# TensorE's order in the scans of a two-layer encoder written out by the program, and the first layer's score products made of 128-row passes

## The chip, the core and the metric

The kernel runs on one core of one Trainium2 chip. The metric is the device time of one execution in microseconds (us), as the median of several runs. Instructions go to engines with queues of their own: TensorE (PE in the profile; its weight loads are PEld), VectorE (DVE), ScalarE (ACT), GpSimd (POOL), and SyncE (SP), which here issues the DMAs.

## The reference: what is computed

Two sequences, 512 and 256 tokens of width 1024, go through a trunk of two layers with shared weights.

- Layer 0 mixes tokens by dilated sliding-window attention (8 heads of 64) beside a short gated convolution. Layer 1 mixes them by RWKV-7 time mixing: 16 heads of 64, a forward and a backward scan, summed.
- Each layer then adds a cross-attention over 256 memory tokens (4 heads of 256) and a SwiGLU of inner width 2816. RMS norms stand before every part and at the end.

The scan that gives layer 1 its shape is, per head and token,

```
S_t = S_{t-1} diag(w_t) + (S_{t-1} a_t) b_t^T + v_t k_t^T ;  o_t = S_t r_t
```

## The kernel before, in words

**Numbers.** Activations lie with features on the 128 partitions and tokens along the free axis. Each fp32 operand of a large product is split into a rounded part `hi` and a remainder `lo`, and a product is three passes on TensorE: hi·hi, hi·lo, lo·hi (`mms`, lines 330 to 341, and `products`, lines 324 to 328).

**Weights outside the scans.** `wcols` (lines 250 to 274) loads up to 2048 weight columns per partition, then splits a tile of 1024 into `whi` on ScalarE (line 269) and `wlo` on VectorE (line 270), with three buffers each.

**The stages, in order.** `mixer0` (layer 0's mixer, lines 617 to 770), `ca` (cross-attention), `ffn`, `mixer1` (layer 1's mixer, lines 1439 to 1486), `ca`, `ffn`. In the profiled execution the scans of `mixer1` lie from 1267 to 2325 us.

**Layer 0's scores.** In `attend` (lines 680 to 725) a head's query and key lie on 64 of the 128 partitions. For each of 4 pairs of heads, 2 heads and 6 blocks of 128 queries (4 of the first sequence with 512 keys, 2 of the second with 256 keys) line 708 makes the three passes over 64 rows. That is 48 sites.

**The scans.** The work of `mixer1_scan` (lines 1041 to 1413) is cut into 12 units, of two heads of the first sequence or four of the second. Four generators do a unit's work in turns: `prep` (decays, keys, norms; its products are line 1073 by `wide` and lines 1025 and 1038 by `head_rsqrt`), `inverse` (the triangular inverses: products of line 1179, then the 32-row products of lines 1223, 1229, 1248 and 1257, with a chain of small VectorE operations between), `scan`, and `tail`. `weave` (line 1535) gives turns in proportion to a count. Beside unit u's scan stand the inverse of unit u+1, the tail of u-1 and the prep of u+2 (line 1404).

**A scan step.** There are 8 steps a unit, 96 in all. `C<-uv,G` and `C<-S,ar` make P; ScalarE copies it to R (line 1328); `C<-R,Xinv` makes U; ScalarE and VectorE copy it to uv (lines 1331 and 1332); `C<-uv,BT` makes Z, which VectorE adds into the state S (line 1343); `y<-G,uv` and `y<-ar,S` make the output. So a step has three round trips from TensorE to another engine and back.

**Fill.** Other dense products (the second sequence's SwiGLU of layer 0, its inputs to the scan, memory keys, the first sequence's output product) are a generator `fill` of some 480 pieces, each of six passes of 256 columns or three of 512. `pour` (line 1279) draws them three times a step.

**What sets TensorE's order.** The program is traced in the order of the turns, and then a scheduler orders each engine's instructions by a simulated timeline; the engine executes that order. Before, the one constraint in the scans is `tc.issue_after`: a piece drawn by `pour` is not issued before the scan's last product traced so far. Everything else may be moved and interleaved.

## Time and profile before

| what | value |
|---|---|
| median of 3 runs (lowest to highest) | 3078.29 us (3075.21 to 3082.93) |
| the profiled execution, its own time | 3090.49 us |
| its span, first to last instruction | 3088.7 us |
| mean granted TensorE clock, share of 2.4 GHz | 0.97 |
| busy share TensorE / weight loads / VectorE / ScalarE / GpSimd | 96 / 81 / 54 / 40 / 21 % |

A line of a group names the source line, engine, operation, output<-inputs, shape and count, then the busy time, the mean length of one, and the idle time just before it with what ended it. Matmuls are pipelined: a 512-column pass is shown some 0.39 us long, but the next starts well before its end. So lengths are not added up; starts are compared. The granted clock has two levels here, 1.0 (2.4 GHz) and 0.5 (1.2 GHz), and a window shows their mean.

### The profile page before, as it was taken

The page shows a single profiled execution, that of the slowest core. Times are in us where ns is not written, and L with a number is a line of the kernel's source. Part 1 is how long each engine was busy: PE and PEld are TensorE (multiplying, and loading weights), DVE is VectorE, ACT ScalarE, POOL GpSimd, SP SyncE. Part 2 cuts the span into 40 slices and gives each one's busy share as a digit, 9 for nine tenths or more (in the row PEclk, how much of TensorE's full clock was granted, in tenths as well). Part 3 has the DMA queues.
Part 4 walks back from the last instruction along what each step waited for, and adds up shares of the span by engine and source line. Part 5 has one row for each costly group of instructions (what it writes and reads, how often), then busy time and mean ns, then how long its engine had stood idle before and what let it go on. Part 6 is the DMA issues. An engine that isn't in the chain of part 4 may idle for free.

```text
span 3088.7 us, 54824 instructions
## 1 busy us (share of the span) xinstructions
PE 2961.8 (96%) x22672; PEld 2487.1 (81%) x22672; DVE 1664.4 (54%) x2762; ACT 1234.2 (40%) x2253; POOL 663.7 (21%) x664
## 2 busy tenths in 40 slices
PE   7999999999999989899989999999999999999997
PEld 6888888888888878787778777777778888888886
DVE  8678646464454486455576455444436464334244
ACT  3232435332222366455556565555345332112112
POOL 3113004020000110232364234444245020000001
PEclk9999999999999989999999899999899999999998
DMA  3114333111265666764435453222352112212211
GB/s 117 49 58 127 102 107 95 65 55 55 97 208 180 210 195 229 237 200 144 139 110 163 137 151 100 76 80 66 107 174 94 53 41 71 66 55 69 69 55 55
DMA packets 349275, 344.46 MB, mean 112 GB/s; under 512 B 40929, under 2 KB 287841, under 8 KB 349025
## 3 DMA queue, kind: packets, MB, share of 16 engines
q1 hardware_dynamic: 349024, 340.96, 34.7%
q8 instruction: 178, 2.92, 0.4%
q14 instruction: 73, 0.59, 0.1%
HBM read 269.06 MB, written 71.83 MB: 110 GB/s over the span
## 4 chain that ended last, share of the span: by engine, by line
PE 81%; DVE 8%; DMA 4%; ACT 3%; issue 2%; POOL 1%; SPq 0%; POOLq 0%; DVEq 0%; ACTq 0%
PE mm L337 22%; PE mm L338 21%; PE mm L339 21%; PE C L1288 3%; PE g L1179 3%; PE sm L328 2%; PE y L1288 2%; PE e L1073 2%; DVE lt L1204 1%; DVE xr L1205 1%; PE py L328 1%; PE mm L328 1%; DMA tlo<-low 1%; DMA traw<-in_ffn_wgu_dram 1%; DVE xs L232 1%
## 5 line engine op out<-in xcount | busy, mean ns | idle before, releaser
L337 PE MATMUL mm<-xs,whi 128*128 128x512 f32 x2128 | 754.0, 356 | 29.4 <-ACT whi L269 11.7
L338 PE MATMUL mm<-xs,whi 128*128 128x512 f32 x2128 | 754.0, 354 | 3.6 <-DVE xs L232 2.7
L339 PE MATMUL mm<-xs,wlo 128*128 128x512 f32 x2128 | 749.5, 352 | 2.4 <-DVE wlo L270 2.3
L269 ACT CAST whi<-wraw 128x1024 fp32r<-128x1024 f32 (+1 forms) x246 | 256.1, 1043 | 781.4 <-PE mm L338 742.9
L337 PEld LDWEIGHTS mm<-xs,whi 128*128 128x128 f32 x2128 | 404.0, 190 | 93.7 <-ACT whi L269 12.3
L339 PEld LDWEIGHTS mm<-xs,wlo 128*128 128x128 f32 x2128 | 402.5, 189 | 62.5 <-DVE wlo L270 4.2
L338 PEld LDWEIGHTS mm<-xs,whi 128*128 128x128 f32 x2128 | 403.6, 190 | 59.3 <-DVE xs L232 3.4
L196 POOL TENSOR_TENSOR acc<-acc,sq 128x768 f32<-128x768 f32 (+2 forms) x72 | 123.2, 1711 | 1388.6 <-issue 896.0
L270 DVE TENSOR_TENSOR wlo<-wraw,whi 128x1024 fp32r<-128x1024 f32 (+1 forms) x246 | 309.3, 1260 | 164.5 <-ACT whi L269 156.3
L338 PE MATMUL mm<-fb,thi 128*128 128x256 f32 (+1 forms) x720 | 235.3, 327 | 1.8 <-DVE fb L229 1.8
L338 PE MATMUL mm<-hid,whi 128*128 128x512 f32 (+1 forms) x528 | 188.6, 358 | 0.0
L337 PE MATMUL mm<-hid,whi 128*128 128x512 f32 (+1 forms) x528 | 186.5, 356 | 1.9 <-ACT hid L228 1.9
L339 PE MATMUL mm<-hid,wlo 128*128 128x512 f32 (+1 forms) x528 | 187.0, 355 | 0.0
L337 PE MATMUL mm<-fb,thi 128*128 128x256 f32 x528 | 166.4, 316 | 6.0 <-ACT thi L298 5.9
L298 ACT CAST thi<-traw 128x512 fp32r<-128x512 f32 (+1 forms) x202 | 122.8, 609 | 115.5 <-PE mm L338 63.7
L339 PE MATMUL mm<-fb,tlo 128*128 128x256 f32 x528 | 156.0, 297 | 8.6 <-POOL tlo L302 4.0
L378 DVE SCALAR_TENSOR_TENSOR u<-mm,rstd 128x768 f32<-128x768 f32 (+1 forms) x44 | 38.4, 873 | 211.6 <-PE mm L339 211.6
L338 PEld LDWEIGHTS mm<-fb,thi 128*128 128x128 f32 x720 | 143.9, 200 | 9.3 <-issue 3.6
L398 DVE TENSOR_TENSOR x<-x,mm 128x512 f32<-128x512 f32 (+2 forms) x56 | 42.4, 762 | 173.6 <-PE mm L339 173.5
L337 PE MATMUL mm<-fa,thi 128*128 128x512 f32 (+1 forms) x304 | 128.9, 426 | 0.8 <-ACT fa L228 0.6
L337 PEld LDWEIGHTS mm<-fb,thi 128*128 128x128 f32 x528 | 105.6, 200 | 17.1 <-ACT thi L298 8.6
L339 PE MATMUL mm<-fa,tlo 128*128 128x512 f32 (+1 forms) x304 | 114.1, 375 | 1.7 <-DMA tlo<-low 1.7
(373 smaller groups left out, 5850.8 us busy)
## 6 DMA issues: line engine op xcount, KB each, us to landing
wraw<-in_ffn_wgu_dram SPq DMA_DIRECT2D x44, 1024.0 KB, 5.1
tlo<-low SPq DMA_DIRECT2D x128, 256.0 KB, 3.2
low<-wlo SPq DMA_DIRECT2D x60, 512.0 KB, 3.2
wraw<-in_ffn_wdown_dram SPq DMA_DIRECT2D x23, 1024.0 KB, 5.2
traw<-in_ffn_wgu_dram SPq DMA_DIRECT2D x56, 256.0 KB, 3.5
wraw<-in_ab_w_in_dram SPq DMA_DIRECT2D x24, 512.0 KB, 3.8
wraw<-in_ca_wkv_dram SPq DMA_DIRECT2D x8, 1024.0 KB, 5.5
kvd<-kv SPq DMA_DIRECT2D x32, 256.0 KB, 2.0
```

The costliest lines, as they stand in the source:

```text
L196: nc.gpsimd.tensor_add(acc, acc, sq)
L269: nc.scalar.copy(hi[:, :, :m], raw[:, :, j:j + m])
L270: nc.vector.tensor_sub(lo[:, :, :m], raw[:, :, j:j + m], hi[:, :, :m].bitcast(F32))
L298: nc.scalar.copy(hi[:, :n], raw[:, :n])
L328: self.nc.tensor.matmul(ps, lhsT=a[u], rhs=b[v], start=k == 0 and j == 0, stop=k == len(pairs) - 1 and j == 2)
L337: nc.tensor.matmul(ps[:, s0:s1], lhsT=wh, rhs=xh[:, s0:s1], start=start and k == 0, stop=False)
L338: nc.tensor.matmul(ps[:, s0:s1], lhsT=wh, rhs=xl[:, s0:s1], start=False, stop=False)
L339: nc.tensor.matmul(ps[:, s0:s1], lhsT=wl, rhs=xh[:, s0:s1], start=False, stop=stop and k == n - 1)
L398: self.nc.vector.tensor_add(self.x[m], self.x[m], ps)
L1073: nc.tensor.matmul(ps[:, c], lhsT=l, rhs=r, start=True, stop=True)
L1179: nc.tensor.matmul(ps[h][:, j, d, :], lhsT=flat(BK[d][lohi[h], c]), rhs=flat(AR[d][lohi[h], c]), start=True, stop=True)
L1288: last[0] = nc.tensor.matmul(o, lhsT=lhsT, rhs=rhs, start=start, stop=False, skip_group_check=True)
```

## The change

- In the scans every TensorE instruction is tied behind the one traced before it (`keep_in_program_order`), so the order of turns and of statements is the order that TensorE executes. `pin` is on only around `mixer1_scan`.
- For that order the generators are cut finer: `head_rsqrt` yields between its sum and its transposes, `prep` yields once more, the scan's transposes of values and keys are apart, `mem_kv` yields before its transposes. `pour` draws two shares between P and U and one at each of the two other places, of 32 a unit instead of 24.
- Layer 0's scores: of a head's query, `hi` stays on the head's 64 rows and the remainder goes by DMA to the other 64 rows; the key's `hi` and `lo` are copied by DMA to both halves. Two passes over 128 rows take the place of three over 64 (the lo·lo term comes in too).
- `wcols` splits a weight tile in two halves with four buffers each (two whole tiles instead of three); a one-row-block load takes 512 columns instead of 1024. `mixer0` draws the weights of the next product ahead of the current one.
- Two tables are moved or shrunk (`gmu`, `rstd`), which is not shown.

```diff
@@ class Net
+    def matmul(self, *args, **kw):
+        return self.pinned(self.nc.tensor.matmul(*args, **kw))
...
+    def pinned(self, ins):
+        if self.pin[0]:
+            self.tc.keep_in_program_order(ins)
+        return ins
...
@@ def wcols
-        W = min(n, 2048 // nk // 128 * 128)
-        cw = min(W, 1024 // nk // 128 * 128)
+        W = min(n, 2048 // nk // 128 * 128 if nk > 1 else 512)
+        cw = min(W, 1024 // max(2, nk) // 128 * 128)
...
-                hi = self.wp.tile([128, nk, cw], F32R, name="whi", bufs=3)
-                lo = self.wp.tile([128, nk, cw], F32R, name="wlo", bufs=3)
-                nc.scalar.copy(hi[:, :, :m], raw[:, :, j:j + m])
-                nc.vector.tensor_sub(lo[:, :, :m], raw[:, :, j:j + m], hi[:, :, :m].bitcast(F32))
+                parts = []
+                for k0 in range(0, nk, -(-nk // 2)):
+                    k1 = min(nk, k0 - (-nk // 2))
+                    hi = self.wp.tile([128, k1 - k0, cw], F32R, name="whi", bufs=4)
+                    lo = self.wp.tile([128, k1 - k0, cw], F32R, name="wlo", bufs=4)
+                    nc.scalar.copy(hi[:, :, :m], raw[:, k0:k1, j:j + m])
+                    nc.vector.tensor_sub(lo[:, :, :m], raw[:, k0:k1, j:j + m], hi[:, :, :m].bitcast(F32))
+                    parts.append((k0, k1, hi, lo))
...
@@ def mem_kv
             if m >= KT:
+                yield
                 p2 = self.sm(4, 128)
@@ def mixer0
+        cols = [1024, *head(0), *keyq(1), 1152, *head(1), *keyq(2), None, *head(2), 1280, *keyq(3), *head(3), None, 1408]
+        made = {}
+        def make():
+            c = cols.pop(0) if cols else None
+            if c is not None:
+                made[c] = next(self.wcols(w_in, 0, 8, c, 128))
...
         def product(col, tag="mm", **kw):
             ps = self.pmm.tile([128, T], F32, name=tag, **kw)
-            self.mm(ps, next(self.wcols(w_in, 0, 8, col, 128)), xs)
+            if col not in made:
+                make()
+            w = made.pop(col)
+            make()
+            self.mm(ps, w, xs)
...
-            hi, lo = self.pair("qk", 8)
-            nc.scalar.copy(hi, z)
-            nc.gpsimd.tensor_sub(lo, z, hi.bitcast(F32))
-            return hi, lo
+            return z
+        def half(z, to, rest):
+            for t, r, rows in zip(to, rest, heads):
+                nc.scalar.copy(t[rows], z[rows])
+                nc.gpsimd.tensor_sub(r[rows], z[rows], t[rows].bitcast(F32))
+        def other(t, h, src):
+            nc.sync.dma_start(t[heads[1 - h]].bitcast(F32), src)
...
         def keys(p, o):
+            z = rotary(proj(512 + p * 128))
+            hi = [self.ph.tile([128, T], F32R, name="qk", bufs=12) for _ in heads]
+            lo = [self.ph.tile([128, T], F32R, name="qk", bufs=12) for _ in heads]
+            half(z, hi, lo)
+            for h, rows in enumerate(heads):
+                for t in (hi[h], lo[h]):
+                    other(t, h, t[rows].bitcast(F32))
...
+            z = rotary(proj(p * 128, 0.125))
+            o["q"] = [self.ph.tile([128, T], F32R, name="qk", bufs=12) for _ in heads]
+            half(z, o["q"], [z, z])
+            for h, t in enumerate(o["q"]):
+                other(t, h, z[heads[h]])
@@ attend
-                        self.products(ps[:, :n], [([a[hs, c:c + 128] for a in q], [a[hs, s0:s1] for a in k])])
+                        for j, kt in enumerate(k[h]):
+                            self.matmul(ps[:, :n], lhsT=q[h][:, c:c + 128], rhs=kt[:, s0:s1], start=j == 0, stop=j == 1)
@@ def head_rsqrt
         nc.scalar.copy(bc, y[:, :8].rearrange("p (t h) -> p t h", h=2).unsqueeze(3).to_broadcast([128, 4, 2, 64]))
+        yield
         out = pool.tile([128, 512], F32, name="e")
@@ mixer1_scan, prep
                 rks.append((c, rk))
+            yield
@@ mixer1_scan, scan
-            def pour():
-                todo[0] += rate[2 + u] / 24
+            def pour(n):
+                todo[0] += n * rate[2 + u] / 32
                 while todo[0] >= 1:
                     todo[0] -= 1
-                    with tc.issue_after(last[0].ins):
-                        next(fill, None)
+                    next(fill, None)
...
-            nxt = ahead(0)
+            uv = values(0)
+            yield
+            bt = keys(0)
             yield
...
-                    pour()
+                    pour(2)
                     R = ph.tile([128, 128], F32, name="R", bufs=1)
...
-                    pour()
+                    if j and i + 1 < NG:
+                        bt2 = keys(i + 1)
+                    pour(1)
                     yield
...
                     if j == 0 and i + 1 < NG:
-                        nxt = ahead(i + 1)
-                    pour()
+                        uv2 = values(i + 1)
+                    pour(1)
...
@@ mixer1_scan
-            weave((part(scan, u), 17), (part(inverse, u + 1), 16), (part(tail, u - 1), 4), (part(prep, u + 2), 12))
+            weave((part(scan, u), 18), (part(inverse, u + 1), 16), (part(tail, u - 1), 5), (part(prep, u + 2), 14))
@@ mixer1
+                    self.pin[0] = True
                     y = self.mixer1_scan(L, rkv, zs, bvs, self.fill(l, f, xsave, rkv, L, zs))
+                    self.pin[0] = False
```

## Rows read from the trace of the kernel before

**Rows 1.** Timeline of TensorE, a dense stretch: start, length, instruction.

```profile
1220.21 0.39 PE L338 MATMUL mm<-xs,whi 128*128 128x512 f32 x1
1220.44 0.39 PE L339 MATMUL mm<-xs,wlo 128*128 128x512 f32 x1
```

**Rows 2.** Windows: us, busy time of each engine, granted clock, DMA share, GB/s.

```profile
0.00:630.00 630.00, 612.12 (x3456) 517.89 (x3457) 422.99 (x738) 223.07 (x344) 119.38 (x84) 1.00 0.28 88
...
1267.00:2325.00 1058.00, 986.59 (x11899) 796.89 (x11897) 558.36 (x1214) 583.38 (x1315) 425.60 (x488) 0.93 0.44 131
```

**Rows 3.** Waits of TensorE, 1267 to 2325 us: us in total, times, longest.

```profile
PE C L1288 <- DVE S L1343: 6.4, 10, 1.3
PE g L1248 <- DVE X L1231: 6.4, 4, 2.4
...
PE C L1288 <- DVE uv L1332: 5.4, 6, 2.0
...
PE y L1288 <- ACT uv L1331: 4.4, 7, 1.3
PE C L1288 <- ACT R L1328: 4.2, 7, 1.1
...
PE mm L181 <- DVE bc L175: 3.1, 2, 2.7
```

**Rows 4.** Groups by line, shapes kept apart: the first layer's scores, line 328.

```profile
L328 PE MATMUL sm<-qk 64*128 64x512 f32 x96 | 30.5, 425 | 0.0
...
L328 PE MATMUL sm<-qk 64*128 64x256 f32 x48 | 10.1, 314 | 0.3 <-DVE mx L711 0.3
```

**Rows 5.** Timeline of TensorE, two score sites.

```profile
228.25 0.62 PE L328 MATMUL sm<-qk 64*128 64x256 f32 x3
228.79 0.50 PE L337 MATMUL mm<-xs,whi 128*128 128x512 f32 x1
...
256.37 0.96 PE L328 MATMUL sm<-qk 64*128 64x512 f32 x3
257.26 0.39 PE L337 MATMUL mm<-xs,whi 128*128 128x256 f32 x1
```

**Rows 6.** Timeline of TensorE in the scans, dense fill and cut runs.

```profile
1630.96 0.28 PE L337 MATMUL mm<-fb,thi 128*128 128x256 f32 x1
1631.08 0.28 PE L338 MATMUL mm<-fb,thi 128*128 128x256 f32 x1
1631.29 1.71 PE L1179 MATMUL g<-ar,bk 64*128 64x128 f32 x16
1632.93 0.34 PE L1288 MATMUL y<-G,uv 128*64 128x64 f32 x4
...
1635.05 0.48 PE L1179 MATMUL g<-ar,bk 64*128 64x128 f32 x2
1635.47 0.39 PE L338 MATMUL mm<-fb,thi 128*128 128x256 f32 x1
1635.69 0.28 PE L339 MATMUL mm<-fb,tlo 128*128 128x256 f32 x1
1635.90 0.71 PE L1179 MATMUL g<-ar,bk 64*128 64x128 f32 x4
```

**Rows 7.** Timeline: first and last run of L1179, then of L1223 to L1257.

```profile
1301.82 0.48 PE L1179 MATMUL g<-ar,bk 64*128 64x128 f32 x2
...
2195.67 2.08 PE L1179 MATMUL g<-ar,bk 64*128 64x128 f32 x10
...
1356.04 1.29 PE L1223 MATMUL g<-X,G 32*32 32x32 f32 x128 [0.63 <-DVE X L1213]
...
2239.58 0.43 PE L1257 MATMUL g<-Xinv,Y 32*32 32x32 f32 x14
```

**Rows 8.** The page, part 5: the split of a weight tile.

```profile
L269 ACT CAST whi<-wraw 128x1024 fp32r<-128x1024 f32 (+1 forms) x246 | 256.1, 1043 | 781.4 <-PE mm L338 742.9
```

**Rows 9.** The page, part 6: DMA issues, KB each, us to landing.

```profile
tlo<-low SPq DMA_DIRECT2D x128, 256.0 KB, 3.2
```

More of the change, by code (lines that the diff above doesn't have):

```diff
@@ L45, in __init__ @@
         self.W, self.seqs = T, SEQS
[L46 removed]
+        self.slots, self.wide, self.pin = None, False, [False]
         self.open_x()
@@ L205, in rstd @@
             for i, s in enumerate(acc):
-                nc.tensor.matmul(ps[:, t:t + 1], lhsT=s[:, t * 128:(t + 1) * 128], rhs=self.ones,
+                self.matmul(ps[:, t:t + 1], lhsT=s[:, t * 128:(t + 1) * 128], rhs=self.ones,
                                  start=i == 0, stop=i == len(acc) - 1)
@@ L327, in products @@
             for j, (u, v) in enumerate(((0, 0), (0, 1), (1, 0))):
-                self.nc.tensor.matmul(ps, lhsT=a[u], rhs=b[v], start=k == 0 and j == 0, stop=k == len(pairs) - 1 and j == 2)
+                self.matmul(ps, lhsT=a[u], rhs=b[v], start=k == 0 and j == 0, stop=k == len(pairs) - 1 and j == 2)
     def mms(self, ps, w, xs, start=True, stop=True):
@@ L336, in mms @@
             for s0, s1 in self.seqs:
-                nc.tensor.matmul(ps[:, s0:s1], lhsT=wh, rhs=xh[:, s0:s1], start=start and k == 0, stop=False)
-                nc.tensor.matmul(ps[:, s0:s1], lhsT=wh, rhs=xl[:, s0:s1], start=False, stop=False)
-                nc.tensor.matmul(ps[:, s0:s1], lhsT=wl, rhs=xh[:, s0:s1], start=False, stop=stop and k == n - 1)
+                self.matmul(ps[:, s0:s1], lhsT=wh, rhs=xh[:, s0:s1], start=start and k == 0, stop=False)
+                self.matmul(ps[:, s0:s1], lhsT=wh, rhs=xl[:, s0:s1], start=False, stop=False)
+                self.matmul(ps[:, s0:s1], lhsT=wl, rhs=xh[:, s0:s1], start=False, stop=stop and k == n - 1)
             if (k + 1) % PIECE[self.W] == 0 and k + 1 < n:
@@ L628, in mixer0 @@
             nc.sync.dma_start(self.rot[i], a["rot"][i])
+        head = lambda p: [2048 + 128 * p, 2560 + 128 * p, 1536 + 128 * p]
+        keyq = lambda p: [512 + 128 * p, 128 * p]
+        cols = [1024, *head(0), *keyq(1), 1152, *head(1), *keyq(2), None, *head(2), 1280, *keyq(3), *head(3), None, 1408]
[5 more added lines that the diff above has]
+        make()
         def product(col, tag="mm", **kw):
             ps = self.pmm.tile([128, T], F32, name=tag, **kw)
-            self.mm(ps, next(self.wcols(w_in, 0, 8, col, 128)), xs)
+            if col not in made:
+                make()
+            w = made.pop(col)
+            make()
+            self.mm(ps, w, xs)
             return ps
@@ L1047, in mixer1_scan @@
         units += [(1, [(p, slice(0, 256)), (p + 1, slice(256, 512))]) for p in range(0, 8, 2)]
-        last, tc = [None], self.tc
         steps = ([(s, s, 0, s, 7 - s) for s in range(8)],
@@ L1072, in wide @@
             for (c, l), r in zip(lhsT, rhs):
-                nc.tensor.matmul(ps[:, c], lhsT=l, rhs=r, start=True, stop=True)
+                self.matmul(ps[:, c], lhsT=l, rhs=r, start=True, stop=True)
             return ps
@@ L1126, in prep @@
                     nkk = kk
-                    rn = self.head_rsqrt(sq, 0.0, 1.0, 1e-24, t6, self.pp)
-                    nc.vector.scalar_tensor_tensor(nkk, kk, -1.0, rn, op0=OP.mult, op1=OP.mult)
+                    rn = []
+                    yield from self.head_rsqrt(sq, 0.0, 1.0, 1e-24, t6, self.pp, rn)
+                    nc.vector.scalar_tensor_tensor(nkk, kk, -1.0, rn[0], op0=OP.mult, op1=OP.mult)
                 yield
@@ L1277, in scan, with values @@
             todo = [0]
-            def pour():
-                todo[0] += rate[2 + u] / 24
+            def pour(n):
+                todo[0] += n * rate[2 + u] / 32
                 while todo[0] >= 1:
                     todo[0] -= 1
-                    with tc.issue_after(last[0].ins):
-                        next(fill, None)
+                    next(fill, None)
             def mm(o, lhsT, rhs, start=False):
-                last[0] = nc.tensor.matmul(o, lhsT=lhsT, rhs=rhs, start=start, stop=False, skip_group_check=True)
-            def ahead(i):
+                self.matmul(o, lhsT=lhsT, rhs=rhs, start=start, stop=False, skip_group_check=True)
+            def values(i):
                 g = st[2 * i:2 * i + 2]
@@ L1381, in tail @@
             yield
-            nc.vector.tensor_mul(y, y, self.head_rsqrt(sq, 64e-5, 1.0 / 64, None, tt, self.pp))
+            rn = []
+            yield from self.head_rsqrt(sq, 64e-5, 1.0 / 64, None, tt, self.pp, rn)
+            nc.vector.tensor_mul(y, y, rn[0])
             for p, c in parts:
@@ L1400, in mixer1_scan @@
         rate = [n * r / sum(f) for n, f in zip(self.fill_len(), FILL) for r in f]
-        weave((part(prep, 0), 12), more(rate[0]))
-        weave((part(inverse, 0), 16), (part(prep, 1), 12), more(rate[1]))
+        weave((part(prep, 0), 14), more(rate[0]))
+        weave((part(inverse, 0), 16), (part(prep, 1), 14), more(rate[1]))
         for u in range(NU + 1):
-            weave((part(scan, u), 17), (part(inverse, u + 1), 16), (part(tail, u - 1), 4), (part(prep, u + 2), 12))
+            weave((part(scan, u), 18), (part(inverse, u + 1), 16), (part(tail, u - 1), 5), (part(prep, u + 2), 14))
         for _ in fill:
```

69 lines of the change are left out of this document (39 added, 30 removed).

## The prediction

> **What bounds the kernel now.** I read the page's busy shares first: TensorE is busy nearly all of the span and no other engine is near it. Busy time of pipelined passes says little: a dense 512-column pass is shown 0.39 us long, but the next starts 0.23 us after it [rows 1]. So the windows by stage came next. In layer 0's mixer the clock is full and TensorE's idle time is small; in the scans, 1267 to 2325 us, TensorE is idle for 1058.0 - 986.6 = 71 us, and its clock is 0.93 on average, which costs (1 - 0.93) x 1058 = 74 us of work not done [rows 2]. The waits say what the 71 us are: many short ones, none of which dominates [rows 3]. They are of three kinds. Round trips of a scan step (S, both uv, R) make 6.4 + 5.4 + 4.4 + 4.2 = 20.4 us in 30 waits, 0.68 us each; products of the inverse wait 6.4 us for X; the fill waits for split weights, and 3.1 us for a norm's spread.
>
> The third loss is in no wait. In the timeline a fill pass of 256 columns starts 0.12 us after the one before, and 16 line 1179 records in one run take 1632.93 - 1631.29 = 1.64 us, 0.10 each. Cut out as two records they take 1635.47 - 1635.05 = 0.42 us instead of 0.21; the fill pass behind them takes 0.22, and the one ahead of the next cut 0.21, instead of 0.12 [rows 6]. So an excursion of two records from the fill and back costs 0.21 + 0.10 + 0.09 = 0.4 us that no wait explains. The scheduler makes many: the timeline of 1267 to 2325 us has line 1179 in 92 separate runs (first and last shown) and the 32-row products in 110 [rows 7].
>
> **The change, part by part.** The sum is made against the profiled execution, 3090.5 us, which is 12.2 us above the median of the runs.
>
> *Layer 0's scores: -16.* There are (96 + 48) / 3 = 48 sites, 32 of 512 columns and 16 of 256 [rows 4]. Three 64-row passes hold TensorE for 257.26 - 256.37 = 0.89 us and 228.79 - 228.25 = 0.54 us [rows 5]. Two 128-row passes at the pitch of dense passes, 0.23 [rows 1] and 0.12 [rows 6], are 0.46 and 0.24. The saving is 32 x 0.43 + 16 x 0.30 = 18.6 us. The lowest it can be is one pass of each site, 32 x 0.23 + 16 x 0.12 = 9.3. The stage is TensorE's: VectorE has 423 of 630 us [rows 2], so it counts. Against it stand 24 DMAs inside the core, one more ScalarE copy and one more GpSimd subtraction for each of 8 keys and queries. GpSimd has 119 of 630 us and ScalarE 223 [rows 2]; both have room. A transfer's nearest price is 3.2 us to landing [rows 9]; for pairs 1 to 3 attention of the pair before hides it, for pair 0 the convolution's products do, unless they have run out: 0 to 5 us. I take 3, so -16, bounds -19 and -4. SP's queue carries the 24 DMAs among loads issued well ahead.
>
> *Weight tiles in halves, drawn ahead: 0.* A split lasts 1.04 us [rows 8]; a stage's first product can start after half of it, some 0.5 us at each of a few starts. Each half pays a start of its own on ScalarE and VectorE, hidden beside TensorE outside the scans. Two tiles of room instead of three leave about one product, 24 passes or more of 0.23 us, to prepare the next; that covers a split. The exception is line 877, which opens three columns at once; with room for two the third starts later. -3 to +6, I take 0.
>
> *Order in the scans, fewer runs: -33.* Laid out in the order of turns, line 1179 makes one run of 16 records for each of 4 turns in 12 units, 48, and the 32-row products one run for each of 4 turns, 48. That removes 44 and 62 runs. 44 x 0.4 = 18 us by the row above. For the 32-row runs no clean pair of rows stands here; the lower end is 0.1 (one slower start), the upper 0.4, and I take 0.25 since many lie beside other small products: 15 us. Bounds -11 (0.1 for each of 106) and -42.
>
> *Order in the scans, waits: -12.* Now every wait holds all that follows, so I count the cover that the new order writes down. Between P and U stand two fill pieces, 12 x 0.12 = 1.4 us; between U and Z one piece, 0.7 us, and on average two turns of the other generators; between Z and the next step the output products and another piece. A round trip that fails now fails by 0.68 us on average [rows 3], so 0.7 to 1.4 us of certain cover should end at least half of them: -10. The inverse's products get a turn or more of distance: -7 from the inverse's waits, of which X is the largest. The weight waits stay: the same buffers feed the fill. New ones: the norm inside `small_low` must now be followed at once by its transposes, +3 by the price of the same helper at the start [rows 3]; and the one bank that `prep` and `tail` share can be asked for in neighbouring turns, +2. Sum -12. Bounds: -45 if all but the weight waits go; above, what the rival below says.
>
> *The clock: -17.* The clock's 74 us follow from the waits. Listing the low stretches behind the idle times over 1 us, about half of the low time (68 of some 140 us at the low level) stands behind waits of steps and inverses. If half of those go, 68 / 2 / 2 = 17 us come back. Bounds -47 (in proportion to all waits that could go, 45 of 71) and 0.
>
> Sum: -16 + 0 - 33 - 12 - 17 = **-78 us**, 3012 against the profile's 3090.5, and 3078.3 - 78 = **3000 us** against the median.
>
> **Where a page and the rows differ.** The Trainium skill (TensorEngine Tiling (Array Packing), section Tiling Modes, under Key Properties) says that changing the tiling mode drains TensorE. The traces agree at both places used above: 64-row passes are slow at their edges in rows 5 and in rows 6. By that rule alone only changes of the active rows or columns would count, and not every broken run. They number 726 in the timeline of the scans and 562 in the new order; at 0.1 us, an estimate from the fill's slower starts, the runs would give -16 instead of -33 and the total 3017.
>
> **The rivals.**
>
> *All waits covered.* If the written order covers every round trip, the terms are -19 - 42 - 45 - 47 = -153: 2925 us. For it: the cover of 0.7 to 1.4 us exceeds the mean wait. Against it: the copies wait in ScalarE's and VectorE's queues behind other work, and those two queues are still ordered by the simulated timeline.
>
> *Waits at the head (slower).* The place is the step's round trips, 96 x 3 = 288. If ScalarE or VectorE come to a copy late, nothing later can pass it now. The price is 0.68 us each [rows 3], and about half as much again in clock. A third of all trips waiting, beyond those that wait today, is 96 x 0.68 x 1.5 = 98 us, against -16 - 33 = -49: 3127 us. It decides from 49 / 1.02 = 48 more waits, one trip in six. For it: VectorE runs 558 of 1058 us and the inverse's chain must fit among the rest [rows 2]; the scheduler chose its order to avoid just these waits in its simulation. Against it: 30 of 288 wait today in an order that was simulated with durations that need not be the chip's, with no cover written down.
>
> *The order hardly changes.* If the scheduler's order was close to the program's, only layer 0's part is left: 3062 us. The cuts of two and four records [rows 6] speak against it.
>
> **How the numbers follow.** The forecast gets 0.55, its own range is 2950 to 3060. All waits covered: 0.16. Order hardly changed: 0.08. Waits at the head: 0.17. The remaining 0.04 is gains and losses that cancel. About 0.3%, 9 us, is what a measurement of this kernel can tell from no change. Faster by more: nearly all of the first, all of the second, most of the third, 0.76. Slower: 0.17. Same: 0.07. The range for 8 in 10 reaches down to the second case's centre, which leaves out 0.07, and up to 3095, which leaves out the larger part of the slow case, 0.13: 2925 to 3095.
>
> **What would show it.** Right: the score sites as pairs of 128-row passes with no slow start behind them; line 1179 in 48 runs of 16; fewer and shorter waits of line 1288; a mean clock in the scans of 0.95 or more; the scans shorter by some 60 us and layer 0's mixer by some 16. Wrong: waits of line 1288 for R, uv or S that together exceed 50 us, a clock at or below 0.93, or a wait for a score's copied half at the first pair. The prediction fails if the scans are as long as before though line 1179 stands in 48 runs: then cuts cost less than the rows say, or new waits took their place.

## The result and the profile after

The changed kernel takes 3119.5 us (median of 4 runs, 3113.7 to 3120.9), the kernel before 3080.6 us in runs beside it: a ratio of 1.0125, 95% interval 1.0105 to 1.0145. It is slower by 39 us, where I had forecast 78 us less. Its profiled execution took 3113.7 us, its span is 3111.9 us, so profile against profile the loss is 23 us; the profiled execution of before lay some 10 us above its median, this one 6 below. Times are medians; one slow run of four of f6_pairs_free_order, 5078.1 us, is left out.

The granted clock of whole runs goes with the two figures. It was 0.970 in the profiled execution of before, where the runs of that kernel recorded with the experiments have 0.974 on average, and 0.971 in this one, where its four runs have 0.967. So the two profiles show the same clock, while over the runs the changed kernel loses up to (0.974 - 0.967) x 3100 = 22 us more to it, an estimate from the clocks of the runs.

The windows of the changed kernel, layer 0's mixer and the scans (us, then busy time of TensorE, weight loads, VectorE, ScalarE, GpSimd, granted clock, DMA share, GB/s):

```profile
0.00:620.00 620.00, 589.53 (x3391) 511.32 (x3392) 434.38 (x798) 238.81 (x412) 132.32 (x91) 0.99 0.32 97
1250.00:2350.00 1100.00, 929.82 (x11918) 754.84 (x11917) 556.03 (x1220) 582.83 (x1319) 428.37 (x489) 0.94 0.42 126
```

Beside [rows 2], TensorE is idle for 170 us in the scans instead of 71, and the clock of the profiled execution is what it was. The waits of TensorE in the same stretch (all its products now carry line 52 and its transposes line 55, the lines of the helpers, so the tiles tell them apart) name the idle time:

```profile
PE C L52 <- ACT R L1396: 41.7, 24, 4.6
PE C L52 <- DVE uv L1400: 33.2, 30, 4.1
PE e L55 <- DVE rs_w L1091: 11.9, 7, 5.3
PE g L52 <- DVE X L1276: 11.1, 6, 8.0
...
PE mm L52 <- ACT thi L313: 9.6, 4, 7.9
PE e L55 <- ACT bc L1096: 8.9, 6, 3.6
```

Against [rows 3], the wait for R has gone from 4.2 us in 7 to 41.7 us in 24, the one for uv from VectorE from 5.4 us in 6 to 33.2 us in 30.

**Where the time went.** I cut every trace at the same two places: the start of the norm that opens the scan stage and the end of the last fill product. Of the stage in between, three things can be counted: the time in which TensorE does nothing, half of its busy time at the low clock level (1.2 GHz, summed from the stretches of the granted clock), and the rest, which is its work at 2.4 GHz.

| us | start of stage | length | idle | low clock, half | rest | behind it |
|---|---|---|---|---|---|---|
| before | 1267.0 | 1065.0 | 71.4 | 66.5 | 927.1 | 756.7 |
| changed | 1250.6 | 1103.7 | 170.2 | 57.5 | 875.9 | 757.7 |
| difference | -16.4 | +38.6 | +98.8 | -9.0 | -51.2 | +1.0 |

-16.4 + 38.6 + 1.0 = 23.2 us, the difference of the spans. So the change shortened TensorE's work more than I had said, and new waits took twice of that back. The low level itself lasted 139.9 us in both stages; its half is 9 us less only because TensorE is idle for more of it.

**Why R comes late.** In a timeline of the changed kernel (start, length, instruction, in brackets the idle time before it and what ended it):

```profile
1833.82 0.39 PE L52 MATMUL C<-S,ar 128*64 128x128 f32 x4
...
1835.31 0.40 PE L52 MATMUL mm<-fb,thi 128*128 128x256 f32 x2
1835.54 0.28 PE L52 MATMUL mm<-fb,tlo 128*128 128x256 f32 x1
1835.91 0.62 ACT L1337 COPY v<-v 128x512 f32<-128x512 f32 x1 [4.59 <-DMA v<-v]
1836.54 2.50 ACT L1304 COPY Xinv<-XL 32x512 f32<-32x512 f32 x4
1839.06 0.69 ACT L1171 ACTIVATE th<-e,half 128x512 f32<-128x512 f32 x1
1839.65 0.26 ACT L1396 COPY R<-C 128x128 f32<-128x128 f32 x1
...
1839.96 0.66 PE L52 MATMUL C<-R,Xinv 128*128 128x64 f32 x4 [4.14 <-ACT R L1396]
```

P is done at 1834.2 us and the fill behind it covers the trip until 1835.8. But ScalarE has stood for 4.59 us before the copy of v, which waits for its DMA; then come four copies of Xinv and a tanh, and R only behind them. In 11 of the 12 units the copy of v stands so ahead of one R, in ten of them with all four copies of Xinv and the tanh, and R starts 3.1 to 5.4 us after P is done. The 11 waits make 32.9 of the 41.7 us. ScalarE's order is still made by the simulated timeline, presumably with v landed sooner (not shown); the order of TensorE is not, so nothing that could run meanwhile is allowed ahead of `C<-R,Xinv`.

### The profile page after: what moved, and what is told of

It reads as the page before. It is cut to its first block, busy times and chain, and to the rows that moved or that the text cites. A ratio compares the mean times of both kernels' runs of the same rounds, so it can differ in the third digit from the quotient of the medians.

```text
span 3111.9 us, 55784 instructions
## 1 busy us (share of the span) xinstructions
PE 2877.7 (92%) x22624; PEld 2437.0 (78%) x22624; DVE 1691.9 (54%) x3008; ACT 1279.3 (41%) x2507; POOL 670.7 (22%) x672
## 5 line engine op out<-in xcount | busy, mean ns | idle before, releaser
L52 PE MATMUL mm<-xs,whi 128*128 128x512 f32 (+1 forms) x4256 | 1132.0, 354 | 14.9 <-ACT whi L281 11.0
L281 ACT CAST whi<-wraw 128x512 fp32r<-128x512 f32 (+1 forms) x492 | 301.5, 616 | 840.4 <-PE mm L52 791.9
L282 DVE TENSOR_TENSOR wlo<-wraw,whi 128x512 fp32r<-128x512 f32 (+1 forms) x492 | 364.8, 743 | 390.1 <-ACT whi L281 352.3
L52 PE MATMUL mm<-hid,whi 128*128 128x512 f32 (+1 forms) x1056 | 282.0, 356 | 2.3 <-ACT hid L236 2.3
L52 PEld LDWEIGHTS mm<-hid,whi 128*128 128x128 f32 x1056 | 186.2, 189 | 31.8 <-ACT hid L236 2.7
L52 PE MATMUL mm<-fa,thi 128*128 128x256 f32 (+1 forms) x416 | 140.1, 387 | 5.0 <-ACT fa L452 3.4
L52 PE MATMUL mm<-o,whi 128*128 128x512 f32 (+1 forms) x512 | 130.1, 342 | 2.8 <-DVE x L590 1.1
L52 PEld LDWEIGHTS mm<-fb,tlo 128*128 128x128 f32 x528 | 106.9, 203 | 8.7 <-DMA tlo<-low 4.8
L52 PEld LDWEIGHTS mm<-hid,wlo 128*128 128x128 f32 x528 | 99.3, 188 | 14.7
L52 PEld LDWEIGHTS mm<-o,whi 128*128 128x128 f32 x512 | 88.3, 189 | 15.9 <-DVE o L237 2.3
L52 PE MATMUL C<-R,Xinv 128*128 128x64 f32 x384 | 58.1, 276 | 41.8 <-ACT R L1396 41.7
```

The lines of the kernel that those rows point to most:

```text
L52: return self.pinned(self.nc.tensor.matmul(*args, **kw))
L281: nc.scalar.copy(hi[:, :, :m], raw[:, k0:k1, j:j + m])
L282: nc.vector.tensor_sub(lo[:, :, :m], raw[:, k0:k1, j:j + m], hi[:, :, :m].bitcast(F32))
```

## The experiments

Ratios are against the kernel before on the same chip. Idle time, low clock and rest are those of the stage, from each kernel's one trace; "clock" is the mean granted clock of all its runs, over the whole execution (before: 0.974), where 0.001 is 3 us; "pairs" is explained under the third question.

| kernel | us | ratio, 95% interval | clock | stage | idle | low | rest | pairs |
|---|---|---|---|---|---|---|---|---|
| changed | 3119.5 | 1.0125 (1.0105 to 1.0145) | 0.967 | 1103.7 | 170.2 | 57.5 | 875.9 | 370 |
| e2_layer0_alone | 3051.1 | 0.9909 (0.9884 to 0.9934) | 0.978 | 1042.6 | 61.5 | 55.0 | 926.1 | 166 |
| e9_weights_alone | 3067.6 | 0.9977 (0.9962 to 0.9993) | 0.977 | 1042.7 | 62.4 | 52.7 | 927.6 | 161 |
| e1_order_free | 3094.8 | 1.0056 (1.0032 to 1.0079) | 0.965 | 1082.2 | 77.5 | 78.7 | 925.9 | 142 |
| e4_pin_alone | 3304.6 | 1.0728 (1.0696 to 1.0760) | 0.936 | 1297.4 | 265.9 | 163.3 | 868.3 | 384 |
| e3_v_on_gpsimd | 3087.1 | 1.0031 (1.0014 to 1.0048) | 0.972 | 1082.1 | 149.8 | 57.0 | 875.3 | 374 |
| e5_two_copies_tied | 3077.0 | 0.9996 (0.9976 to 1.0016) | 0.973 | 1067.7 | 137.2 | 56.0 | 874.5 | 374 |
| e6_scalar_in_order | 3161.0 | 1.0287 (1.0240 to 1.0335) | 0.955 | 1153.4 | 177.7 | 105.0 | 870.7 | 378 |
| e7_scalar_vector_in_order | 3212.2 | 1.0433 (1.0397 to 1.0469) | 0.949 | 1206.9 | 208.2 | 130.5 | 868.2 | 376 |
| g1_uv_on_scalar | 3062.6 | 0.9941 (0.9919 to 0.9963) | 0.974 | 1050.8 | 131.6 | 43.0 | 876.2 | 376 |
| f2_cover_for_uv | 3111.8 | 1.0132 (1.0097 to 1.0167) | 0.968 | 1111.1 | 158.6 | 78.7 | 873.8 | 378 |
| f3_norm_yield | 3092.7 | 1.0067 (1.0041 to 1.0093) | 0.969 | 1081.9 | 149.8 | 61.0 | 871.1 | 378 |
| f4_cover_yield_priority | 3134.6 | 1.0198 (1.0164 to 1.0232) | 0.959 | 1129.3 | 156.3 | 106.1 | 867.0 | 376 |
| f1_runs_by_priority | 3037.6 | 0.9889 (0.9851 to 0.9927) | 0.977 | 1027.2 | 63.2 | 45.4 | 918.5 | 127 |
| f8_pairs_apart | 3148.4 | 1.0217 (1.0186 to 1.0248) | 0.963 | 1125.6 | 154.2 | 79.5 | 891.9 | 140 |
| f6_pairs_free_order | 3046.2 | 0.9877 (0.9840 to 0.9913) | 0.978 | 1038.8 | 86.7 | 50.2 | 902.0 | 370 |
| f5_pairs_and_priority | 3038.8 | 0.9868 (0.9844 to 0.9892) | 0.977 | 1029.0 | 91.5 | 50.2 | 887.3 | 382 |
| g2_free_pairs_tied | 3063.9 | 0.9935 (0.9914 to 0.9956) | 0.972 | 1051.4 | 107.8 | 57.8 | 885.8 | 372 |

### First question: which part of the change costs?

**e1_order_free.** The finer cuts stay, the order of TensorE is given back to the scheduler.

```diff
-                    self.pin[0] = True
+                    self.pin[0] = False
...
-                    next(fill, None)
+                    with tc.issue_after(last[0].ins):
+                        next(fill, None)
```

> The changed kernel with TensorE's order in the scans left to the scheduler again (fill pieces tied only behind the scan's last product, as before); the finer cuts and all of layer 0's part stay. Theory A (the fixed order itself costs: TensorE stands at each product whose operand a copy on ScalarE or VectorE brings late, and nothing later may pass): its idle time in the scans falls from 170 us to near the 71 us of before, and the time to 3060 us (3045 to 3080). Theory B (the finer cuts and the other shares of the turns cost, not the order): it stays at 3105 to 3130 us.

Measured 3094.8 us, between the two theories. The fixed order itself costs 25 us net (3119.5 - 3094.8; 21 by the ratios); in the trace, rest and idle time are back near their values of before (925.9 and 77.5 us), as theory A has it. That the time doesn't follow is mostly the clock: 0.965 over the runs.

**e2_layer0_alone.** `mem_kv`, `head_rsqrt`, `mixer1_scan` and `fill_len` are those of before; all else is the change's. **e9_weights_alone.** The same, and the three 64-row passes of before besides, so that of the change only the weight tiles and the moved tables are left.

> The scans as before, everything outside them as changed (128-row passes, halved weight tiles, weights drawn ahead). By the prediction's term and theory A: 16 us faster than before, 3064 us (3055 to 3075), with the scans as long as before. Theory C (the halves and the copies give back what the passes save): 3078 us or more, and then the scans cost less than theory A says.

> The scans of before and the three 64-row passes of before; only the weight tiles in halves, the weights drawn ahead and the moved tables of the change are in. My prediction had 0 for this part (-3 to +6) and -16 for the two 128-row passes. If that split holds, the first norm of the scan stage starts at 1264 to 1270 us (before 1267.0, with the passes 1246.8) and the time is 3070 to 3085 us. If the halves carry part of the gain, the start is under 1260. The scan stage itself has the code of before: if the order of the simulated timeline is the reason why it was 22 us shorter with the passes (1042.6 against 1065.0 us), its length here may be anything between 1040 and 1080.

The first product of the stage tells the layer's part. In the timelines of e9_weights_alone and of e2_layer0_alone:

```profile
1264.72 0.50 PE L52 MATMUL mm<-ones,acc 128*128 128x1 f32 x4
```

```profile
1246.84 0.50 PE L52 MATMUL mm<-ones,acc 128*128 128x1 f32 x4
```

Weights: 1267.0 - 1264.7 = 2.3 us. Passes: 1264.7 - 1246.8 = 17.9 us. Two score sites of the changed kernel show why:

```profile
236.32 0.41 PE L52 MATMUL sm<-qk 128*128 128x256 f32 x2
236.56 0.38 PE L55 MATMUL sm<-ident,e 128*128 128x128 f32 x2
...
253.85 0.63 PE L52 MATMUL sm<-qk 128*128 128x512 f32 x2
254.31 0.28 PE L52 MATMUL mm<-xs,whi 128*128 128x256 f32 x1
```

254.31 - 253.85 = 0.46 us and 236.56 - 236.32 = 0.24 us, where three passes held 0.89 and 0.54 [rows 5].

The stage of e9_weights_alone, whose scans have the code of before, is 22 us shorter than in the profile of before at the same rest (927.6 and 927.1). All of it is idle time and clock. Part is the execution that was profiled (the ratio allows -2 to -12 us for the whole kernel); the order that the simulation makes moves a little whenever anything around it changes. So idle time and clock of a free order are known to some 15 us here, the rest to about 2. The starts of the kernels with all that the change does ahead of the stage lie between 1245.3 and 1250.6 us, so the 2.3 us of the weights are no more than the scatter.

The 44 us of e1_order_free over e2_layer0_alone are idle time (+16) and clock (+24 in the traces), in the same rest. The clock is more than the scatter of one trace here: 0.965 over 10 runs beside 0.978 over 4, up to 40 us. Which of the finer cuts brings this wasn't tried.

**e4_pin_alone.** The coarse scans of before with TensorE's order fixed.

```diff
+                    self.pin[0] = True
...
-                    with tc.issue_after(last[0].ins):
-                        next(fill, None)
+                    next(fill, None)
```

> The scans of before, cut as coarsely as before, with TensorE's order fixed; outside the scans as changed. Theory A: without the finer cuts the fixed order waits more often than in the changed kernel, since sums and transposes of one norm then stand next to each other and a step has 1.4 pieces at each place: 3140 to 3220 us. Theory B: the cuts are what costs, so 3090 us or less.

3304.6 us: 253 more than the same kernel with its order free, and beyond what I expected. The stage has 204 us more idle time, 108 more of low clock and 58 less of the rest. The waits of TensorE:

```profile
PE e L55 <- ACT bc L1095: 83.3, 23, 5.3
PE e L55 <- ACT uv L1359: 70.2, 48, 3.7
```

The first is the norm whose transposes follow their sum at once, the second the keys' transposes, which need the PSUM bank that ScalarE is still emptying for uv. In the changed kernel, which has yields at both places, 11.9 + 8.9 us are left of the norm's and 2.3 us of the bank's. So the finer cuts are needed for a fixed order; how much each does wasn't taken apart.

### Second question: whose waits are the 99 us?

**e3_v_on_gpsimd**, **e5_two_copies_tied** and **e6_scalar_in_order** take hold of ScalarE's queue at three widths.

```diff
-                nc.scalar.copy(v2[:, b, 0, :], v[:, ::-1, ::-1])
+                nc.gpsimd.tensor_copy(v2[:, b, 0, :], v[:, ::-1, ::-1])
```

> The changed kernel with one copy moved: the reversal of v at the head of each scan goes from ScalarE to GpSimd. In the changed kernel ScalarE stands 32 us in 14 waits at this copy for its DMA, with four copies of the inverse and the step's copy of P queued behind it. Theory A: the waits of TensorE for that copy (41.7 us) fall by at least half and the time by 20 to 40 us, to 3080 to 3100 us. If the lateness comes from the four copies of the inverse and the tanh themselves, not from the DMA at their head, 0 to 8 us.

```diff
-                nc.scalar.copy(v2[:, b, 0, :], v[:, ::-1, ::-1])
+                tc.keep_in_program_order(nc.scalar.copy(v2[:, b, 0, :], v[:, ::-1, ::-1]))
...
-                nc.scalar.copy(X[qs, :, qs], XL[qs])
+                tc.keep_in_program_order(nc.scalar.copy(X[qs, :, qs], XL[qs]))
```

> The changed kernel with five ScalarE copies of a unit (the reversed values v and the four blocks of Xinv) tied behind the ScalarE instruction traced before each. Theory A, the waits come from ScalarE's queue, in which the simulated timeline puts these copies ahead of R: the 41.7 us of waits for R fall under 20 us, TensorE's idle time in the scan stage from 170 to about 140, time 3085 to 3100 us. Theory B, the round trips are too short for any order of ScalarE: waits for R stay near 40 us and the time within 3110 to 3125 us.

Taking the copy of v off ScalarE gives 32 us back and halves the wait for R (20.7 us in 24), as its first theory has it; tying five copies (0.62 us each) to their place in the program gives 42 us, and the whole loss against the kernel before is gone. The wait of TensorE for R in e5_two_copies_tied:

```profile
PE C L52 <- DVE uv L1401: 30.8, 26, 3.0
PE C L52 <- ACT R L1397: 14.2, 16, 2.7
```

It fell from 41.7 to 14.2 us and the stage's idle time by 33 us. Theory A holds; the time is 8 us below its range.

e6_scalar_in_order and e7_scalar_vector_in_order tie every instruction of the scan's generators on ScalarE, and then on VectorE too, behind the one traced before it.

> The changed kernel with every ScalarE instruction of the scan's four generators (not those of the fill) tied behind the one traced before it, so that ScalarE's queue follows the same order as TensorE's. Theory A (the queues of the two engines were ordered by different rules): waits for R under 15 us, idle time of the stage 120 us or less, time 3050 to 3085 us. Theory B: ScalarE now holds its own queue at the head, waits move to other tiles (th, Y, BT), idle time 160 or more, time 3110 us or more.

> As the kernel before it, with VectorE's instructions of the four generators in program order as well. Theory A: waits for uv on VectorE (33.2 us) fall under 15 too, idle time 90 us or less, time 3010 to 3060 us. Theory B: the inverse's chain of small VectorE operations now stands whole before uv and S in each turn, waits for uv and S grow over 50 us, time 3130 us or more.

Both theories A fall here. The wait for R in e6_scalar_in_order, and three of e7_scalar_vector_in_order:

```profile
PE C L69 <- ACT R L47: 52.5, 32, 4.3
```

```profile
PE C L69 <- DVE S L47: 54.5, 23, 4.1
PE C L69 <- ACT R L47: 48.6, 29, 4.4
PE e L72 <- ACT v L47: 31.2, 9, 18.4
```

Each queue now stops at its own head: the wait for uv does fall, to 6.3 us in e7_scalar_vector_in_order, but others grow. Waits are the smaller part, though. Beside the changed kernel the stage of e6_scalar_in_order has 8 us more idle time and 48 more of low clock (0.955 over the runs beside 0.967), that of e7_scalar_vector_in_order 38 and 73. With nearly the same idle time, 170 and 178 us, the low clock takes 57.5 and 105.0 us, so idle time alone doesn't set it; what does stays open. What helped among these is a queue that can still choose, with the few late instructions held back.

**g1_uv_on_scalar** asks the same of the second wait, uv on VectorE, in e5_two_copies_tied.

```diff
-                    nc.vector.tensor_copy(uv[lohi[1], j, 1, :], U[lohi[1]])
+                    nc.scalar.copy(uv[lohi[1], j, 1, :], U[lohi[1]])
```

> The kernel with the two copies tied (3077 us; 30.8 us of waits for uv on VectorE, 14.2 for R on ScalarE) with VectorE's half of uv copied by ScalarE, behind ScalarE's own half. Theory A, uv is late because VectorE stands in one of the long operations of its queue (the chain of the inverse, the decays' scan) when U is done: the waits for uv fall under 15 us although ScalarE now makes two copies in a row, time 3055 to 3070 us. Rival, the trip itself lacks cover whatever engine copies: waits for uv on ScalarE 25 us or more, time 3075 us or more.

3062.6 us, and this wait in its trace:

```profile
PE C L52 <- ACT uv L1401: 11.3, 19, 1.5
```

So the wait for uv was VectorE's queue. Little of it came back as time without waits: R (17.1 us), X (17.1) and S (9.6) now wait 14 us more together, and idle time falls from 137.2 to 131.6 us only. Of the 17 us by which the stage is shorter 13 are low clock, so the time is in the range of theory A in part by luck. In VectorE's queue uv stood behind the inverse's chain and the decays, as here in the changed kernel, where `C<-uv,BT` starts 4.05 us late:

```profile
1894.98 1.19 DVE L1268 TENSOR_TENSOR xr<-xr,lt 128x54 f32<-128x54 f32 x1
...
1896.59 0.68 DVE L1209 TENSOR_TENSOR bk<-th,cu 128x512 f32<-128x512 f32 x1
1897.30 0.29 DVE L1400 COPY uv<-C 64x128 f32<-64x128 f32 x1
...
1897.65 0.69 PE L52 MATMUL C<-uv,BT 128*64 128x64 f32 x8 [4.05 <-DVE uv L1400]
```

**f2_cover_for_uv**, **f3_norm_yield** and **f4_cover_yield_priority** leave the late copies and give TensorE more to do beside them.

```diff
                         bt2 = keys(i + 1)
-                    pour(1)
+                    pour(2)
...
                         uv2 = values(i + 1)
-                    pour(1)
```

> The kernel with the two copies tied (3077 us) with the third share of fill of a step moved from behind Z to between U and Z: shares 2, 2, 0 instead of 2, 1, 1. Theory A, the trip over uv lacks cover: waits for uv (30.8 us in 26) fall to half or less, waits for S rise from 4 to at most 15, idle time of the stage from 137 to about 115, time 3045 to 3065 us. Rival: VectorE comes so late to uv that no piece of fill covers it, or S takes the waits over: idle time 130 or more, time 3070 us or more.

```diff
         yield
+        yield
         out = pool.tile([128, 512], F32, name="e")
```

> The kernel with the two copies tied (3077 us) with one more turn between a head norm's sum and its transposes. Waits of the transposes for rs_w and bc (13.3 and 8.5 us) should fall under 8 together, if a turn of the others has work for TensorE; the time 3060 to 3072 us. If a turn covers nothing here, they stay above 15 and the time within 3072 to 3082.

f4 has both, and asks for the copies of R and uv at the highest priority.

> The two edits before together, and the copies of R and uv given to the scheduler at the highest priority. If the waits of a fixed order can be covered one by one, idle time falls to about 100 us, the stage to 874 + 100 + 55 = 1030 us and the time to 3035 to 3050 us, level with layer 0's part alone in a free order (3051). If a new wait takes the place of each one covered, idle time stays above 120 and the time above 3060.

All three are slower than the kernel they start from (3077.0 us). The waits aimed at did fall: uv to 15.0 us in 13 in f2_cover_for_uv, rs_w and bc to 4.8 us together in f3_norm_yield, uv to 3.6 in f4_cover_yield_priority. Others rose: R (20.0), S (13.6) and the values' transposes for v (16.8) in the first, R (23.2) and products into the tile e, whose bank VectorE still reads for y (21.9), in the second. Cover written at one trip seems to be cover taken from another. Idle time rose by 21, 13 and 19 us beside e5_two_copies_tied, and the low clock by 23, 5 and 50: in the slowest, f4_cover_yield_priority, the clock is most of the loss (0.959 over the runs beside 0.973).

No fixed order made up for what it costs: the best, g1_uv_on_scalar, is at 0.9941 of before, and e2_layer0_alone, whose scans are left as they were, at 0.9909.

### Third question: what did the fixed order gain?

The rest fell by 51 us, where cuts priced at 0.4 and 0.25 us had promised 33. **f1_runs_by_priority** removes cuts alone, in the free order of e2_layer0_alone.

```diff
+                with self.tc.high_priority():
                     for j in range(2):
                         for d in range(2):
                             c = st[2 * i + j][d]
...
+            with self.tc.high_priority():
                 for v in range(16):
```

> The scans of before, their order left to the simulated timeline, with layer 0's and the weights' part of the change (as e2_layer0_alone, 3051 us) and one more edit: the products of the inverse (L1179 and the 32-row ones of before) are given to the scheduler at the highest priority, so that a run that has begun is cut less often. TensorE changes its kind of work 989 times in the scans instead of 1069. Theory A, each cut costs by itself: the change from 1066 to 877 took 51 us of TensorE's full-speed time, 0.27 us each, so 80 fewer give -22 us in the part that is neither idle nor low clock (926 to about 905), waits about as they were, and 3025 to 3040 us. Rival: the 51 us came from something else in the fixed order; the part stays within 5 us of 926 and the time at 3045 us or above.

The time is in the range of theory A, but not by its price. In the trace the rest went from 926.1 to 918.5 us. The 32-row products went from 107 runs to 64 and hold TensorE for 59.9 us instead of 66.2 (start to the next start, without idle time, the low level halved): 6.3 / 43 = 0.15 us a cut. L1179 still stood in 94 runs. Then what made 51 us? The timeline of before has the answer, in runs of L1179 that stand one behind the other:

```profile
1704.89 1.16 PE L1179 MATMUL g<-ar,bk 64*128 64x128 f32 x16
1708.71 1.16 PE L1179 MATMUL g<-ar,bk 64*128 64x128 f32 x8
1710.23 1.16 PE L1179 MATMUL g<-ar,bk 64*128 64x128 f32 x8
```

Sixteen records take 1.16 us and eight take 1.16 us (a product of the program is two records here). The two heads of a unit lie on the two halves of the rows. Where records of both are at hand, they start in pairs, 7 ns apart, and the next pair 0.105 us later; where the eight of one head come alone, each takes 0.11 us by itself. I counted these pairs: 166 of 384 before, 370 in the changed kernel. L1179 holds TensorE for 83 us before and 58 after, `y<-G,uv`, whose run of eight records is cut in two less often, for 42 and 33, and the 32-row products for 67 and 57: 45 of the 51 us. The 204 more pairs at 0.11 us are 23 of them.

**f8_pairs_apart** takes the pairs apart in the fixed order and leaves the runs whole.

```diff
-                for j in range(2):
-                    for d in range(2):
-                        c = st[2 * i + j][d]
-                        for h in range(2):
+                for h in range(2):
+                    for j in range(2):
+                        for d in range(2):
+                            c = st[2 * i + j][d]
```

> The changed kernel, its order as fixed as before, but in each run of the inverse's 16 products (L1179 of the kernel before) the eight of the first head stand ahead of the eight of the second, so that no two neighbours lie on different halves of the rows. Theory P (pairs on the two halves run side by side, 0.105 us a pair; that is what the fixed order gained): a run of 16 takes 1.64 us or more instead of 1.09, 48 x 0.55 = +26 us in the part that is neither idle nor low clock (876 to about 902); the time is 3125 to 3150 us, less where the longer runs cover a wait. Theory C (cuts): the runs are as uncut as before, so nothing changes, 3110 to 3122 us.

+29 us, and a run of its timeline:

```profile
1714.08 1.71 PE L52 MATMUL g<-ar,bk 64*128 64x128 f32 x16
```

1.71 us for the same 16 records. Order within an uncut run does decide it, as theory P has it and theory C doesn't: L1179 holds TensorE for 80 us instead of 58. The pairs are not all apart; in most runs three starts still lie within 7 ns of the one before, 140 in all. The rest has 16 us more, not 26, the low clock 22 more and idle time 16 less, so that the time is in the range of theory P is partly the clock. The two heads also write two PSUM banks, and no run here takes the halves of the rows and the banks apart.

**f6_pairs_free_order** and **f5_pairs_and_priority** make the pairs in a free order. In the order of before a bank of one head came free ahead of the other's, and its eight products went alone; one tile of two banks frees both at once.

```diff
-                ps = [self.pg.tile([128, 2, 2, 128], F32, name=f"g{h}") for h in range(2)]
+                ps = self.pg.tile([128, 2, 2, 2, 128], F32, name="g")
+                ps = [ps[:, h] for h in range(2)]
```

> The scans of before in the scheduler's own order with layer 0's part (3051 us), but the two PSUM banks of the two heads are one tile, so that the products of both heads become free to start at the same time. Theory P: pairs rise from 166 to over 300 of 384, the part that is neither idle nor low clock falls from 926 by some 25 us, time 3015 to 3035 us. Theory C: the number of runs in the scans hardly changes (1035 against 1069), so at most -10 us: 3040 to 3055 us.

> Both: one tile for the two heads' banks and the inverse's products at the highest priority, order otherwise free. Theory P: f1_runs_by_priority (3038 us) less 25 to 35 us: 3000 to 3015 us, the part that is neither idle nor low clock at about 885, idle time at 60 to 75 as in the free order. If a run that must be whole holds up the scan's steps as in the fixed order, idle time rises to over 100 and the time is 3035 us or more.

Pairs 370 and 382, rest -24 us (926.1 to 902.0) and -31 us (918.5 to 887.3), as theory P has it. Yet the time hardly moved: 3046.2 us beside 3051.1, and 3038.8 beside 3037.6; by the ratios 10 and 6 us less, within their intervals. The windows of the stage in f1_runs_by_priority and f5_pairs_and_priority show where it went:

```profile
1248.90:2276.00 1027.10, 963.89 (x11927) 785.23 (x11926) 560.69 (x1221) 587.33 (x1322) 430.16 (x491) 0.95 0.44 135
```

```profile
1247.10:2276.10 1029.00, 937.48 (x11927) 758.66 (x11926) 564.50 (x1222) 583.10 (x1321) 432.18 (x492) 0.95 0.44 135
```

TensorE is busy 26 us less in the same length. **g2_free_pairs_tied** (f5 with the ties of e5) asked whether ScalarE's late copies hold it.

> The free order with pairs and priority (3039 us, idle time 91.5 us) with the copies of v and Xinv tied behind what is traced before them on ScalarE. If the idle time that took back the gain of the pairs is made by ScalarE's late copies, as in the fixed order, it falls to 75 us or less and the time is 3015 to 3028 us. If it comes from the trips of the steps themselves, now that less other work lies beside them, it stays above 85 and the time within 3030 to 3048.

They don't: idle time rose to 107.8 us and the time to 3063.9, outside both ranges; the free order presumably had its own use for the place of these copies. What takes the pairs' gain in a free order stays open; the idle time is spread over many short waits. One rival is in the edit itself: it also gives the 32-row products their PSUM out of the one tile, so a bank no longer comes free by itself. That wasn't tried apart.

The fastest of these, f1_runs_by_priority, f6_pairs_free_order and f5_pairs_and_priority, beat both kernels: 0.9889, 0.9877 and 0.9868 of before, where the change is at 1.0125.

## Why the prediction was wrong, step by step

- **Layer 0's scores, -16:** right. 17.9 us by e9 and e2, and 16.4 with the weights in the changed kernel's own start, each good to some 3 us; the pitch of 0.23 and 0.12 us a pass was the right price.
- **Weights, 0:** right; 2.3 us earlier in the traces, which is within -3 to +6 and within the scatter.
- **Fewer runs, -33:** the counts were right (L1179 in 46 runs of 16, two of 15 and two of 1, the 32-row products in 48 runs), the sign and the rough size too, but the price was of the wrong thing. I divided 1.64 us by 16 records [rows 6] and took 0.10 us as what a record costs; in that run only three pairs start together, and 0.11 us can buy two. The term measured -51, beyond my bound of -42: 26 for L1179 against 18, mostly pairs and not cuts; 10 for the 32-row products against 15 (0.15 us a cut against 0.25); and 15 that my sum did not have, 9 of them `y<-G,uv`.
- **Waits, -12:** this is the step that failed. It measured +99. I counted cover on TensorE (1.4 us of fill between P and U) against the mean length of today's waits, 0.68 us [rows 3]. But a wait is only the part of a copy's lateness that TensorE had nothing else to do in, and its order had been chosen freely. A copy's lateness is set by what stands ahead of it in ScalarE's or VectorE's queue, 3.8 us for R (0.62 + 2.50 + 0.69), and no cover of 0.7 to 1.4 us reaches that. I had named these queues as the case against "all waits covered" and then didn't look into them. The trace of before has the same copies ahead of R:

```profile
1827.24 0.39 PE L1288 MATMUL C<-S,ar 128*64 128x128 f32 x4
...
1830.12 2.50 ACT L1241 COPY Xinv<-XL 32x512 f32<-32x512 f32 x4 [2.64 <-DVE XL L1230]
1830.88 1.07 PE L1248 MATMUL g<-X,G 32*32 32x32 f32 x54 [2.35 <-DVE X L1231]
1832.64 0.27 ACT L1328 COPY R<-C 128x128 f32<-128x128 f32 x1
1832.96 1.12 PE L1288 MATMUL C<-R,Xinv 128*128 128x64 f32 x4 [1.01 <-ACT R L1328]
```

R starts 5.0 us after P is done, but TensorE put fill and products of the inverse in between, and 1.01 us is all that shows as a wait for R. Before, R starts over 2 us late in 10 of 96 steps, though it is waited for in 7, for 1.1 us at most; in the changed kernel it starts so late in 15.

- **The clock, -17:** wrong too. The low level was to shrink with the waits; it lasted 139.9 us in both traces, the -9 is idle time within it, and over the runs the clock is lower (0.967 beside 0.974, up to +22 us). Nor does it follow idle time alone: 170 us of it go with 57.5 us of low clock here, 178 with 105.0 in e6.
- **The rival "waits at the head", 3127:** it happened, at its place (R and uv). Its price was off in both factors: some 41 more waits of the two kinds instead of 96, but 1.4 us each ((41.7 + 33.2) / 54) instead of 0.68, and nothing through the clock in these two traces. That its 3127 lies near 3119.5 is in part luck.

My own test in the prediction, over 50 us of waits for R, uv or S, was met with 75 for R and uv alone, and so was the last one: L1179 in 48 turns, scans not shorter, new waits in place of the cuts. The range ended at 3095 because I gave this rival 0.17; with two queues left to a simulation and the third taken from it, that was too little.

## What to carry to other kernels

An order fixed on one engine is only as good as the queues it waits for: before fixing it, list for each handover what stands ahead of the copy on the other engine, and hold back the few long or DMA-fed instructions there (five copies a unit were worth 42 us). Don't fix the other queues whole, and read the granted clock of several runs beside the waits: here it was at times the larger term. And price a product by its start-to-start time in the company in which it runs: here products of two heads on different rows of the array are cheap as neighbours and dear apart. Freeing their PSUM banks together makes the pairs (370 of 384), but in the free order it took 24 us off TensorE's work and hardly anything off the time.

## What the runs showed of the hardware

Two 64-row records on the two halves of the rows start 7 ns apart, and the next two 0.105 us later; eight of one half alone take as long as sixteen in pairs (1.16 us each), and sixteen with the halves mostly apart 1.71 us. The Trainium skill (TensorEngine Tiling (Array Packing), section Key Properties) says that tiles of the array operate independently and can run products in parallel. The traces agree, with the limit that the two halves write two PSUM banks here. In the prediction I had cited the rule beside it, on the drain at a change of mode, which prices the term at -16; pairs were not in my sum.
